# Ordering the start of an MLP's up projection by hand: features, operand sums and the first column pair of a Strassen-Winograd product

## The chip, the cores and the metric

One core of a Trainium2 chip runs the whole program. The metric is device microseconds of one execution. All matrix products are three matmuls each in a split format (see below), so that fp32 data keeps its precision.

## The reference, cut to what matters

A two-layer backbone over 1024 latent tokens and 256 context tokens, width 1024. Layer 0 mixes by differential attention, layer 1 by a bidirectional state-space layer with a gated linear unit (GLU). After every mixer stands a squared-ReLU MLP:

```python
x = x + g1 * rmsnorm(y_lat, norm_g[i, 1])
h = rmsnorm(x, norm_g[i, 2]) * (1.0 + s2) + sh2
x = x + g2 * rmsnorm(sqrelu_mlp(h, mlp_w1[i], mlp_w2[i]), norm_g[i, 3])

def sqrelu_mlp(h, w1, w2):
    return jnp.einsum('btf,fd->btd', jnp.square(jax.nn.relu(jnp.einsum('btd,df->btf', h, w1))), w2)
```

The change is in layer 1, where the context stream is no longer needed: the end of the GLU, the second norm, and the start of `h @ w1` (1024 tokens, 1024 to 4096).

## The kernel before, in words

**Formats.** `split` makes two fp32r halves of an fp32 tile: the high half on ScalarE (a copy, line 137), the low half as the difference on VectorE or GpSimd (line 138). `mm3` (lines 130 to 134) multiplies high by high, high by low and low by high.

**Tokens and columns.** Tokens come in two groups of 512 (g = 0, 1). The normalised activations are turned to features by rows: for each block k of 128 features, four TensorE transposes into one PSUM bank (line 315), a scaling with adaLN scale and shift on VectorE (320) or ScalarE (318), and a split (321, line 138 on GpSimd by default). The result is `hT[g]`, eight blocks each. The 4096 columns come in 32 columns f of 128. Columns 0 to 3 are computed directly (`conventional`: 8 blocks by 3 matmuls for each column and group). The other 28 go in 14 pairs p = 2 to 15 by a Strassen-Winograd scheme: 7 products of 4 blocks (12 matmuls) in place of 8. Its operands on the token side are sums of blocks of `hT`: T1 and T3, T2, and T4, which overwrites the first half of `hT[1]`. On the weight side they are four sums (S1 to S4).

**Order of a pair.** The products are A11·B11, S1·T1, S2·T2, S4·B22, S3·T3, A12·B21, A22·T4, in this order. A11·B11, S2·T2, S3·T3 and A22·T4 accumulate in one PSUM bank (P), S1·T1 and S4·B22 in another (R), A12·B21 in a third (Q). After A11·B11, S1·T1 and S2·T2 ScalarE copies the bank's state out (line 1428) before the next product is added to it. After the others VectorE adds the copy and squares (1432, 1433), or ScalarE takes ReLU and square (1397, 1398). The blocks of the result go to DRAM (Ad), and GpSimd forms four sums of them for the down projection (`sums`, lines 2086 to 2092).

**Scheduling.** Outside hand-ordered sections a scheduler decides at compile time the order of instructions on each engine, from the text's order as rank and a model of the times. Inside `with self.manual():` TensorE, VectorE, ScalarE and GpSimd each issue the section's instructions in the order of the text; where other instructions fall between them stays with the scheduler, and DMAs (all on SP's queue) are the scheduler's too. In before, this stage is all the scheduler's. `stages` and `advance` put the steps of the norm (`finish`, lines 2027 to 2045) between columns in the text.

**The stage.** `glu_done(1)` ends the GLU of the second group: norms, residual, norm, and the features. In before `second_group` (1334) emits for each i of 4 the features i and i + 4 and then the sums (1341 to 1350) that make T1, T3 and T2 of block i. `mlp1_up` (2063) does columns 0 to 3 for group 0, then loads and splits the same weights again for group 1 (2095 to 2103), then `last_sum` (1364) makes T4, four blocks of three VectorE sums and a split, then the pairs follow. `pair_weights` (1400) makes the weight sums and splits of a pair on VectorE and ScalarE; its scratch tile comes from a ring of two that `last_sum` uses too.

Of the kernel before, what the change touches and what calls it, by code (L numbers as in the profile page):

```python
# [70 lines left out]
class Prog:  # L71
# [236 lines left out]

    def to_feature(self, tiles, A, B, hi, lo, banks, tmps, k, eng=None, act=False):

        nc = self.nc
        b = banks.next()
        n = 128 * len(tiles)
        for i, t in enumerate(tiles):
            nc.tensor.transpose(b[:, 128 * i : 128 * i + 128], t[:, 128 * k : 128 * k + 128], self.ident)
        t = tmps.next()[:, 0:n]
        if act:
            nc.scalar.activation(t, b[:, 0:n], AF.Identity, scale=A[:, k : k + 1], bias=B[:, k : k + 1])
        else:
            nc.vector.tensor_scalar(t, b[:, 0:n], A[:, k : k + 1], B[:, k : k + 1], ALU.mult, ALU.add)  # L320
        self.split(hi[:, k, :], lo[:, k, :], t, eng or nc.gpsimd)
        return t
# [17 lines left out]
    def phase_v(self):  # L340
# [1039 lines left out]
    def halves(self, src, slot):  # L1380
        self.split(slot[:, 0], slot[:, 1], src)
        return slot
# [640 lines left out]
    def glu_done(self, g, y1, G, xs, tmps, tb):  # L2023
        nc = self.nc
        A, B = self.modc[:, 1, 4, 0], self.modc[:, 1, 3, 0]

        def finish(t, x):
            y, r = y1[t], [None, None]
            self.dma(x, self.xb[0].rearrange("(c t) d -> t c d", t=8)[t])

            def s0():
                r[0] = self.rms2(y, 4.0 * EPS)

            def s1():
                nc.vector.scalar_tensor_tensor(y, y, r[0], G, ALU.mult, ALU.mult)
                (nc.gpsimd if t % 2 else nc.vector).tensor_tensor(y, x, y, ALU.add)
                self.dma(self.xc[t], y)

            def s2():
                r[1] = self.rms2(y)  # L2040

            def s3():
                nc.scalar.activation(y, y, AF.Copy, scale=r[1])

            self.stages((s0, s1, s2, s3), 1)

        tiles = range(4 * g, 4 * g + 4)
        for t, x in zip(tiles, xs):
            finish(t, x)
        feature = lambda k, tmps: self.to_feature([y1[t] for t in tiles], A, B, *self.hT[g], tb, tmps, k, act=k % 2 == 1)  # L2050
        if g == 0:
            self.stages([lambda k=k: feature(k, tmps) for k in range(8)])
            return
        self.second_group(feature, Ring([self.fv(x, 512) for x in (40, 36, 38, 32, 34)]), 0)

# [7 lines left out]
    def mlp1_up(self):  # L2063
        nc = self.nc
        slots = [self.rv(x, 2, 512) for x in (56, 60, 64, 68, 72, 48, 52)] + [self.hv(64 + 4 * i, 2, 512) for i in range(4)]
        raw1 = Ring([self.wv(2 * i, 512) for i in range(4)])
        ring = Ring(slots[:8])
        banks = [0, 1, 2, 4, 5, 6, 7]
        mb = Ring([self.bank(i) for i in banks])
        ft, st = Ring([self.fv(2 * i, 512) for i in range(16)]), Ring([self.fv(32 + 2 * i, 512) for i in range(5)])  # L2070
        ss = Ring([self.fv(x, 512) for x in (42, 44)])
        put = lambda src: self.halves(src, ring.next())
        B = self.blocks()
        kept = {}

        def emit(p, j, g, t):
            kept[p, j, g] = t
            if (j, g) != (0, 1):
                self.dma(self.Ad[{(0, 0): 0, (1, 0): 5, (1, 1): 6}[j, g]][p], t)
            self.advance(2)  # L2080

        def sums(p, i):
            tt, a = nc.gpsimd.tensor_tensor, lambda j, g: kept[p, j, g]
            t = kept[p, i] = st.next()
            if i == 1:
                tt(t, a(0, 1), a(1, 1), ALU.add)
            elif i == 2:
                tt(t, kept[p, 1], a(0, 0), ALU.subtract)
            elif i == 3:
                tt(t, a(1, 0), kept[p, 2], ALU.subtract)  # L2090
            else:
                tt(t, a(0, 0), a(0, 1), ALU.subtract)
            self.dma(self.Ad[i][p], t)

        for g in range(2):
            if g:
                self.advance()
            for f in range(4):
                w = [put(r) for r in self.load1(1, f, raw1)]
                b, t = mb.next(), ft.next()  # L2100
                self.conventional(b, w, B, g)
                self.square(t, b)
                emit(f // 2, f % 2, g, t)
        self.last_sum(B, ss)
        ring = Ring(slots)
        for p in range(2, 16):
            if p == 15:
                ring = Ring(slots[3:7] + slots[:3])
            w = self.pair_weights([self.load1(1, 2 * p + j, raw1) for j in range(2)], put, ss.next(), False)
            if p == 15:  # L2110
                self.banks1 = [x for x in range(8) if x not in [banks[(mb.i + 1 + k) % 7] for k in range(3)]]
                self.mlp1_start()

            def out(j, g, t):
                emit(p, j, g, t)
                for i in {(0, 1): (), (1, 1): (1,), (0, 0): (2, 4), (1, 0): (3,)}[j, g]:
                    sums(p, i)

            self.pair_products(w, B, mb, [ft.next() for _ in range(4)], out)
            if p in (2, 3):  # L2120
                for i in (1, 2, 4, 3):
                    sums(p - 2, i)

    def mlp1_start(self):
# [235 lines left out]
```

## Time and profile before

| | |
|---|---|
| Time, three runs | 2892.81, 2894.29, 2899.42 us; median 2894.29 |
| The profiled execution's own time | 2899.15 us |
| Its span, first to last instruction | 2897.4 us |
| Mean granted TensorE clock | 0.982 |
| TensorE busy | 2747.0 us (95%), 15225 matmuls |
| VectorE busy | 2026.9 us (70%) |
| ScalarE busy | 1362.4 us (47%) |
| GpSimd busy | 1063.2 us (37%) |
| From 2263 to 2317 us: TensorE, VectorE, ScalarE, GpSimd busy | 42.32, 44.69, 30.31, 23.43 us of 54 |

The views of the profile used are the page's shares by engine, a table of busy time by stretch (us from the span's start, with the granted clock in a column), rows of single instructions in order of time, and the chain that ended last. A row of the timeline gives start, duration (both us), engine, line, operation, what is written from what, shape and count. In brackets stand the engine's idle time before it and what ended that idle time. DVE is VectorE, ACT ScalarE, POOL GpSimd, PE TensorE's matmuls; tiles are named by their pool (PS is PSUM, H, R, F and W are SBUF regions).

### The profile page before, as it was taken

The numbers are of one execution on the slowest core, as the hardware profiler recorded it, in microseconds if no ns is written. First come the engines' busy times: TensorE is split into PE (matmuls) and PEld (weight loads), VectorE is DVE, ScalarE is ACT, GpSimd is POOL, SyncE is SP. The second block draws the span as 40 slices with busy tenths as digits, with TensorE's granted clock in tenths as the row PEclk, the third lists the DMA queues.
The fourth block names the chain that finished last, engine by engine and source line by source line (L and its number), as shares of the span: only waits on it lengthen the run. The fifth ranks groups of instructions, "written<-read, shape, count | busy, mean of one in ns | idle before, by whom it ended". The sixth has DMA issues, their size and how long they took to land. (4 is left out here: it accounts for less than half of the span.)

```text
span 2897.4 us, 43677 instructions
## 1 busy us (share of the span) xinstructions
PE 2747.0 (95%) x15225; PEld 2296.1 (79%) x15225; DVE 2026.9 (70%) x2960; ACT 1362.4 (47%) x2555; POOL 1063.2 (37%) x923
## 2 busy tenths in 40 slices
PE   7999999999899999999999999789899899999999
PEld 4687888888787887878877778688788688878887
DVE  5456778878873667666788777899533787658466
ACT  3425555555654743333444435477344643344443
POOL 3314666666663600000110012699121543336324
PEclk9999999999999999999999999899999999999999
DMA  9955555555836468885899987579743254467544
GB/s 299 303 172 169 151 170 171 176 162 167 252 89 189 125 207 305 292 305 189 288 288 288 263 240 233 169 218 297 235 139 109 73 171 160 158 219 243 164 134 142
DMA packets 452010, 588.43 MB, mean 203 GB/s; under 512 B 60622, under 2 KB 297420, under 8 KB 448588
## 3 DMA queue, kind: packets, MB, share of 16 engines
q1 hardware_dynamic: 451788, 585.63, 64.1%
q8 instruction: 120, 1.97, 0.3%
q14 instruction: 102, 0.84, 0.1%
HBM read 398.47 MB, written 182.82 MB: 201 GB/s over the span
## 5 line engine op out<-in xcount | busy, mean ns | idle before, releaser
L132 PE MATMUL PS<-H 128*128 128x512 f32 x1048 | 413.8, 396 | 6.8 <-ACT H L137 3.9
L133 PE MATMUL PS<-H 128*128 128x512 f32 x1048 | 411.7, 393 | 0.0
L134 PE MATMUL PS<-H 128*128 128x512 f32 x1048 | 410.2, 392 | 0.0
L132 PE MATMUL PS<-H,R 128*128 128x512 f32 (+1 forms) x836 | 309.3, 375 | 0.7 <-ACT H L137 0.7
L133 PE MATMUL PS<-H,R 128*128 128x512 f32 (+1 forms) x836 | 304.9, 365 | 4.1 <-POOL H L138 4.1
L134 PE MATMUL PS<-H,R 128*128 128x512 f32 (+1 forms) x836 | 303.7, 364 | 0.0
L132 PEld LDWEIGHTS PS<-H 128*128 128x128 f32 x1048 | 198.4, 189 | 53.0 <-issue 4.9
L134 PEld LDWEIGHTS PS<-H 128*128 128x128 f32 x1048 | 198.3, 189 | 42.1 <-issue 0.4
L133 PEld LDWEIGHTS PS<-H 128*128 128x128 f32 x1048 | 198.7, 190 | 41.3 <-issue 1.0
L137 ACT ACTIVATE R<-W 128x512 fp32r<-128x512 f32 (+1 forms) x199 | 138.8, 705 | 181.7 <-PE PS L133 115.3
L546 ACT ACTIVATE F<-F,stat 128x1280 f32<-128x1280 f32 x128 | 174.3, 1362 | 100.6 <-DVE F L536 100.4
L132 PE MATMUL PS<-R,H 128*128 128x512 f32 x532 | 213.3, 403 | 1.6 <-ACT R L137 1.6
L133 PE MATMUL PS<-R,H 128*128 128x512 f32 x532 | 210.3, 395 | 0.0
L134 PE MATMUL PS<-R,H 128*128 128x512 f32 x532 | 208.5, 396 | 0.0
L137 ACT ACTIVATE H<-U 128x640 fp32r<-128x640 f32 x216 | 132.7, 676 | 148.4 <-PE PS L133 119.7
L138 DVE TENSOR_TENSOR H<-W,H 128x512 fp32r<-128x512 f32 (+1 forms) x137 | 126.9, 937 | 99.8 <-ACT H L137 99.8
L138 DVE TENSOR_TENSOR H<-U,H 128x640 fp32r<-128x640 f32 x216 | 166.4, 806 | 39.9 <-ACT H L137 38.9
L536 DVE TENSOR_SCALAR_CACHE_REDUCE F<-PS 128x1280 f32<-128x1280 f32 x128 | 185.2, 1483 | 8.1 <-PE PS L523 7.9
L138 DVE TENSOR_TENSOR R<-W,R 128x512 fp32r<-128x512 f32 (+1 forms) x164 | 146.7, 902 | 61.3 <-ACT R L137 54.1
L583 POOL TENSOR_SCALAR R<-F 128x256 fp32r<-128x256 f32 (+1 forms) x128 | 127.8, 999 | 148.8 <-ACT F L582 130.9
L133 PEld LDWEIGHTS PS<-H,R 128*128 128x128 f32 x836 | 161.0, 193 | 26.8 <-POOL H L138 5.9
L132 PEld LDWEIGHTS PS<-H,R 128*128 128x128 f32 x836 | 160.2, 192 | 26.5 <-issue 4.1
(501 smaller groups left out, 6843.4 us busy)
## 6 DMA issues: line engine op xcount, KB each, us to landing
W<-in_mlp_w SPq DMA_DIRECT2D x184, 256.0 KB, 3.2
U<-Aa SPq DMA_DIRECT2D x108, 320.0 KB, 4.2
Aa<-FU SPq DMA_DIRECT2D x91, 320.0 KB, 5.3
Ad<-F SPq DMA_DIRECT2D x112, 256.0 KB, 2.4
W<-Ad SPq DMA_DIRECT2D x112, 256.0 KB, 2.9
FU<-in_mlp_w SPq DMA_DIRECT2D x32, 512.0 KB, 5.9
Ta<-FU SPq DMA_DIRECT2D x16, 1024.0 KB, 4.3
recd<-U SPq DMA_DIRECT2D x64, 256.0 KB, 5.0
```

The source lines that it names most:

```text
L132: mm(out, ah, bh, start=first, stop=False, **kw)
L133: mm(out, ah, bl, start=False, stop=False, **kw)
L134: mm(out, al, bh, start=False, stop=last, **kw)
L137: self.nc.scalar.activation(hi, src, AF.Copy)
L138: (lo_eng or self.nc.vector).tensor_tensor(lo, src, hi.bitcast(F32), ALU.subtract)
L536: ts(p[c], self.PS[:, 1280 * c : 1280 * c + 1280], 1.0, None, ALU.mult, ALU.min, accum_out=sm[:, c : c + 1])
L546: nc.scalar.activation(p[c], p[c], AF.Exp, bias=sm[:, c : c + 1], scale=-1.0, accum_out=sn[:, 0:1] if c else s0[:, u + 1 : u + 2])
L583: nc.gpsimd.tensor_scalar(hi, t, 1.0, 0.0, ALU.mult, ALU.add)
```

## The change

Columns 0 to 3 of all tokens and pair 2 become one stretch of text, most of it ordered by hand.

- The weights of columns 0 to 3 are loaded and split once and kept in eight slots for both groups. Columns 0 to 2 of group 0 are multiplied ahead of the ordered section, column 3 inside it, between the first transposes of group 1.
- In the ordered section group 1's features come one after the other, 0 to 7. All are scaled on ScalarE, and their low halves are made on VectorE. Two features behind each, the products of block k for all four columns are issued, into four banks. From feature 4 on, T1 of block k − 4 and the fp32 sums for T2 and T3 are made; the splits of T2 come after the last feature.
- Then come pair 2's weights, ReLU and square of group 1's four columns, the splits of T3, `last_sum`, and pair 2's products with their evacuations; there the section ends.
- Rings of slots and tiles are reordered to fit. `second_group` stays for the first MLP only.

```diff
-        feature = lambda k, tmps: self.to_feature([y1[t] for t in tiles], A, B, *self.hT[g], tb, tmps, k, act=k % 2 == 1)
+        feature = lambda k, tmps: self.to_feature([y1[t] for t in tiles], A, B, *self.hT[g], tb, tmps, k,
+                                                  nc.vector if g else None, g == 1 or k % 2 == 1)
...
-        self.second_group(feature, Ring([self.fv(x, 512) for x in (40, 36, 38, 32, 34)]), 0)
+        self.feature1 = feature
...
-        for g in range(2):
-            if g:
-                self.advance()
-            for f in range(4):
-                w = [put(r) for r in self.load1(1, f, raw1)]
-                b, t = mb.next(), ft.next()
-                self.conventional(b, w, B, g)
-                self.square(t, b)
-                emit(f // 2, f % 2, g, t)
-        self.last_sum(B, ss)
-        ring = Ring(slots)
+        first = []
+        for f in range(4):
+            w, b = [put(r) for r in self.load1(1, f, raw1)], mb.next()
+            if f < 3:
+                self.conventional(b, w, B, 0)
+            first.append((w, b, ft.next()))
+            self.advance(2)
+        self.advance()
+        ring = Ring(slots[8:] + slots[0:8:2] + slots[1:8:2])
+        load = lambda p: [self.load1(1, 2 * p + j, raw1) for j in range(2)]
+        sched = self.manual()
+        sched.__enter__()
+        w = self.up_second(B, first, [mb.next() for _ in range(4)], [ft.next() for _ in range(4)], emit, ss,
+                           lambda: self.pair_weights(load(2), put, ss.next(), False))
         for p in range(2, 16):
...
+            if p > 2:
+                w = self.pair_weights(load(p), put, ss.next(), False)
...
             self.pair_products(w, B, mb, [ft.next() for _ in range(4)], out)
+            if p == 2:
+                sched.__exit__(None, None, None)
...
+    def up_second(self, B, first, banks, tiles, emit, ss, weights):
...
+        def t1(k):
+            t = more.next()
+            tt(t, raw[k], b11[k][0], ALU.subtract)
+            tt(t, t, b11[k][1], ALU.subtract)
+            self.split(T[1][0][:, k], T[1][1][:, k], t)
+            tt(raw[k], raw[k + 4], raw[k], ALU.subtract)
+            tt(raw[k + 4], raw[k + 4], t, ALU.subtract)
...
+        for k in range(8):
+            one(k)
+            for i in ((0, 1, 2), (3, 4, 5), (6, 7))[k] if k < 3 else ():
+                products(i, 0, [first[3][0:2]])
+            if k < 4:
+                relu(k)
+            if k > 3:
+                done(k - 4)
+            if k > 1:
+                products(k - 2)
+            if k > 3:
+                t1(k - 4)
+        halves(2, lambda k: raw[k + 4])
+        products(6)
+        products(7)
+        w = weights()
+        for f in range(4):
+            self.square(tiles[f], banks[f])
+            emit(f // 2, f % 2, 1, tiles[f])
+        halves(3, lambda k: raw[k])
+        self.last_sum(B, ss)
+        return w
```

`one(k)` makes feature k, `relu` and `done` are ReLU and square of group 0's columns, `products(k)` are 12 matmuls, and `halves(j, ...)` splits the four blocks of Tj.

More of the change, by code (lines that the diff above doesn't have):

```diff
@@ L2069, in mlp1_up @@
         mb = Ring([self.bank(i) for i in banks])
-        ft, st = Ring([self.fv(2 * i, 512) for i in range(16)]), Ring([self.fv(32 + 2 * i, 512) for i in range(5)])
+        ft, st = Ring([self.fv(2 * i, 512) for i in [0, 1, 2, 3, *range(8, 16), 4, 5, 6, 7]]), Ring([self.fv(32 + 2 * i, 512) for i in range(5)])
         ss = Ring([self.fv(x, 512) for x in (42, 44)])
         put = lambda src: self.halves(src, ring.next())
+        self.T = {j: (self.rv(16 * j - 16, 4, 512), self.rv(16 * j - 8, 4, 512)) for j in (1, 2, 3)}
         B = self.blocks()
@@ L2108, in mlp1_up @@
                 ring = Ring(slots[3:7] + slots[:3])
-            w = self.pair_weights([self.load1(1, 2 * p + j, raw1) for j in range(2)], put, ss.next(), False)
+            if p > 2:
+                w = self.pair_weights(load(p), put, ss.next(), False)
             if p == 15:
@@ L2122, in mlp1_up, with one, relu, done @@
                     sums(p - 2, i)
+    def up_second(self, B, first, banks, tiles, emit, ss, weights):
+        act, tt = self.nc.scalar, self.nc.vector.tensor_tensor
+        raw, free = {}, Ring([self.fv(x, 512) for x in (40, 36, 38, 32, 34, 8, 10, 12)])
+        more = Ring([self.fv(14, 512), self.fv(42, 512)])
+        b11 = [[t[:, k].bitcast(F32) for t in self.hT[0]] for k in range(4)]
+        T = self.T
+        def one(k):
+            raw[k] = self.feature1(k, free)
+        def relu(f):
+            act.activation(first[f][2], first[f][1], AF.Relu)
+        def done(f):
+            act.activation(first[f][2], first[f][2], AF.Square)
+            emit(f // 2, f % 2, 0, first[f][2])
+        def products(k, g=1, todo=[(f[0], b) for f, b in zip(first, banks)]):
+            x = B[f"B{k // 4 + 1}{g + 1}"]
+            for w, b in todo:
+                ah, al = (shaped(w[k // 4][:, j], (4, 128))[:, k % 4] for j in range(2))
+                self.mm3(b, ah, al, x[0][:, k % 4], x[1][:, k % 4], k == 0, k == 7)
+        def t1(k):
[5 more added lines that the diff above has]
+            tt(raw[k + 4], raw[k + 4], t, ALU.subtract)
+        def halves(j, src):
+            for k in range(4):
+                self.split(T[j][0][:, k], T[j][1][:, k], src(k))
+        for k in range(8):
[20 more added lines that the diff above has]
+        return w
     def mlp1_start(self):
```

## The prediction

> **What bounds the kernel.** I read the page first, then the busy time by stretch around the change, then the order of instructions there on TensorE, VectorE, ScalarE and GpSimd.
>
> ```profile
> span 2897.4 us, 43677 instructions
> ...
> PE 2747.0 (95%) x15225; PEld 2296.1 (79%) x15225; DVE 2026.9 (70%) x2960; ACT 1362.4 (47%) x2555; POOL 1063.2 (37%) x923
> ...
> core 0: us, PE busy (x) PEld busy (x) DVE busy (x) ACT busy (x) POOL busy (x), PEclk, DMA share, GB/s
> 2270.00:2285.00 15.00, 9.41 (x46) 6.80 (x47) 14.92 (x19) 10.65 (x20) 7.35 (x5) 1.00 0.57 175
> 2285.00:2300.00 15.00, 13.06 (x47) 9.88 (x46) 15.00 (x21) 7.40 (x13) 6.77 (x4) 0.77 0.00 1
> 2300.00:2315.00 15.00, 11.68 (x39) 9.05 (x38) 10.19 (x15) 7.43 (x14) 8.02 (x2) 0.77 0.10 33
> 2345.00:2375.00 30.00, 30.00 (x134) 24.86 (x133) 24.32 (x28) 11.19 (x20) 17.43 (x12) 1.00 0.57 199
> ```
>
> TensorE bounds the whole (95%). At 2345 it is full: 134 matmuls in 30 us. From 2270 to 2315 it issues 46, 47 and 39 in 15 us each, while VectorE is busy without a break until 2300, and the granted clock falls to 0.77. So in this stage VectorE is the bound, and the stage is the one that the change rewrites. TensorE's own rows:
>
> ```profile
> 2268.67 0.40 PE L134 MATMUL PS<-H 128*128 128x512 f32 x1
> ...
> 2283.91 0.66 PE L315 MATMUL PS<-ident,F 128*128 128x128 f32 x4 [3.36 <-DVE F L320]
> ...
> 2291.74 0.99 PE L315 MATMUL PS<-ident,F 128*128 128x128 f32 x4 [1.92 <-ACT F L318]
> ...
> 2306.47 0.80 PE L133 MATMUL PS<-H,R 128*128 128x512 f32 x1 [3.32 <-POOL H L138]
> ...
> 2307.49 0.63 PE L133 MATMUL PS<-H,R 128*128 128x512 f32 x1
> 2307.91 0.63 PE L134 MATMUL PS<-H,R 128*128 128x512 f32 x1
> ...
> 2312.18 0.50 PE L134 MATMUL PS<-H 128*128 128x512 f32 x1
> ...
> 2319.36 0.39 PE L132 MATMUL PS<-R 128*128 128x512 f32 x1
> ...
> 2322.08 0.39 PE L132 MATMUL PS<-R 128*128 128x512 f32 x1
> ```
>
> The first token half's four columns are done at 2268.9. At 2319.36 pair 2's second product (S1·T1, 12 matmuls) starts, at 2322.08 its third (S2·T2): 2.72/12 = 0.227 us each, so its first product began at 2316.64. Between 2268.9 and 2316.64 (47.7 us) TensorE has 96 matmuls (21.8 us) and eight sets of four transposes (0.44 us each by the chain's row below, 3.5 us) to do: 25.3 us. **22.4 us are lost here**: three long idles, shorter ones, and after each long one a stretch of matmuls 0.42 us apart (2307.49, 2307.91) instead of 0.227, after the last idle until 2312.18, 5.7 us that cost 2.7.
>
> **What the change removes.** The weights of the four columns are loaded and split once: 8 loads, 8 ScalarE and 8 VectorE instructions fall away. Eight low halves leave GpSimd for VectorE, four scalings leave VectorE for ScalarE. What GpSimd cost:
>
> ```profile
> 2263.36 1.29 POOL L138 TENSOR_TENSOR H<-F,H 128x512 fp32r<-128x512 f32 x1 [2.67 <-ACT H L137]
> ...
> 2284.59 1.60 POOL L138 TENSOR_TENSOR H<-F,H 128x512 fp32r<-128x512 f32 x1 [2.62 <-ACT H L137]
> 2284.97 1.77 DVE L1371 TENSOR_TENSOR F<-F,H 128x512 f32<-128x512 f32 x1
> ...
> 2297.51 8.91 POOL L138 TENSOR_TENSOR H<-F,H 128x512 fp32r<-128x512 f32 x1 [3.60 <-ACT H L137]
> ...
> 2299.20 0.68 DVE L1344 TENSOR_TENSOR F<-F,H 128x512 f32<-128x512 f32 x1
> 2299.80 0.68 DVE L138 TENSOR_TENSOR R<-F,R 128x512 fp32r<-128x512 f32 x1
> ```
>
> A VectorE sum beside a GpSimd one takes 1.77 instead of 0.68 us (1.1 lost), and one GpSimd subtraction took 8.91 us while VectorE ran sums every 0.60 us; TensorE's 3.32 us idle before 2306.47 waited for it. [...]
>
> **What it puts in.** Each engine now issues this stage, through pair 2, in the order of the text. That order is the point. I follow it with these durations:
>
> ```profile
> 2257.12 1.16 ACT L2043 ACTIVATE F<-F,stat 128x1024 f32<-128x1024 f32 x1 [0.36 <-POOL stat L144]
> ...
> 2259.07 0.44 PE PS L315 x4
> ...
> 2276.37 0.60 PE L315 MATMUL PS<-ident,F 128*128 128x128 f32 x4
> ...
> 2295.63 0.76 ACT L318 ACTIVATE F<-PS,modc 128x512 f32<-128x512 f32 x1
> 2296.29 0.62 ACT L137 ACTIVATE R<-W 128x512 fp32r<-128x512 f32 x1
> ...
> 2262.13 0.63 ACT L137 ACTIVATE R<-W 128x512 fp32r<-128x512 f32 x1 [1.63 <-DMA W<-in_mlp_w]
> ...
> 2262.79 0.69 DVE L138 TENSOR_TENSOR R<-W,R 128x512 fp32r<-128x512 f32 x1 [1.56 <-ACT R L137]
> ...
> 2270.00 0.64 ACT L1398 ACTIVATE F<-F 128x512 f32<-128x512 f32 x1
> 2270.52 0.60 ACT L1397 ACTIVATE F<-PS 128x512 f32<-128x512 f32 x1
> 2270.99 0.64 ACT L1398 ACTIVATE F<-F 128x512 f32<-128x512 f32 x1
> ...
> 2316.84 0.60 ACT L1428 ACTIVATE F<-PS 128x512 f32<-128x512 f32 x1 [0.58 <-PE PS L134]
> ```
>
> *Start.* The second group's last row is normalised at 2257.12 + 1.16 = 2258.3. TensorE is covered beyond that by columns 0 to 2: column 3 (24 matmuls, 5.4 us) now comes later, so the first transposes start at 2268.9 − 5.4 = 2263.5, 5.2 us after their input. Without that cover the wait would show.
>
> *Features.* Transposes 0 to 3 (1.8 us), column 3 (5.4) and the second half's products 0 and 1 (24 matmuls, 5.4) put transposes 4 at 2276.1. TensorE hardly waits up to here: one feature asks 0.66 + 0.52 + 0.48 us of ScalarE and 0.60 of VectorE, TensorE 2.5 or more. Feature 4's low half starts on VectorE after the transposes (0.60), scaling (0.76) and high half (0.62): 2278.1.
>
> *VectorE from there.* Up to the last sum for T4 it has four low halves, four times five instructions for T1 (k = 0 to 3; the sums for T2 and T3 are among them), four halves of T2, seven halves and four sums of pair 2's weights, four halves of T3, and 15 of last_sum: 58 × 0.60 = 34.8 us. Where a sum is split at once, VectorE waits for ScalarE's high half: 0.63 + 0.69 + two gaps of 0.03, less the 0.60 that is counted, 0.8 us. That is four times for T1, three for S1, S2 and S4, three for T4: 8.0 us. Before T3's halves ScalarE has the four squares of the second half: 8 instructions, 0.47 or 0.52 apart, 4.0 us. VectorE still has about 0.9 of low halves when they begin and needs a high half of 0.6 after them: 3.7 us idle. End: 2278.1 + 34.8 + 8.0 + 3.7 = 2324.6.
>
> *The new wait.* Pair 2's S2·T2 adds into the bank of A11·B11, so it waits for ScalarE's copy of that bank (L1428). In the text the copy stands behind last_sum. ScalarE must first do T4's fourth high half: 2324.6 + 0.1 + 0.5 = 2325.2, copy 0.6, S2·T2 at 2325.9. Queued behind it on TensorE are the other products of pair 2; behind the halves on VectorE the pair's evacuations. TensorE needs S2·T2 much earlier: the second half's products end near 2276.1 + 1.8 + 16.3 = 2294.2 (four more sets of transposes, 72 matmuls), A11's low half starts at 2278.1 + 28 × 0.60 + 4 × 0.8 = 2298.1, and A11·B11 and S1·T1 at first at the low clock end near 2305. About 20 us of TensorE are free there; those earlier stalls are hidden in it.
>
> [...]
>
> *What fills the wait.* Pair 3 stands outside the ordered section, and such work does get between ordered instructions: a copy of the next phase (L271) went ahead of the last instruction of the phase before, which is ordered by hand too (L1889).
>
> ```profile
> 2063.86 0.28 DVE L271 COPY adat<-PS 96x128 f32<-96x128 f32 x1
> 2064.05 0.68 DVE L1889 SCALAR_TENSOR_TENSOR H<-PS,H 128x512 fp32r<-128x512 f32 x1
> ...
> 2312.34 1.60 POOL L2086 TENSOR_TENSOR F<-F 128x512 f32<-128x512 f32 x1 [5.92 <-ACT F L1398]
> ...
> W<-in_mlp_w SPq DMA_DIRECT2D x184, 256.0 KB, 3.2
> ```
>
> Of pair 3 only A11·B11 and A12·B21 can run early: their weights need no sum, the raw buffers are free near 2303 and 2307 and filled 3.2 us later, and their halves fit the 0.8 us waits on VectorE. S1 can't: its scratch tile is last_sum's third. So 24 matmuls, 5.4 us, are brought forward. One sum for the Ad tiles (L2086) has both tiles and a free buffer by then and may run on GpSimd beside last_sum: 1.1 us on VectorE, so S2·T2 at 2327.0.
>
> *The low clock.* No row shows the clock after so long a wait with some work in it. Bounds: nothing, if the fill keeps the clock up, and 2.7 us, as after 2306.47. I take 2.4, near the upper end, as the granted clock is 0.77 in both stretches that hold the idles of 1.9 to 3.4 us. [...]
>
> **The sum.** S2·T2 later: 2327.0 − 2322.1 = +4.9. Low clock +2.4. Pair 3 brought forward −5.4. Net +1.9 us. TensorE is full behind this in before, and the rest isn't changed but for which slots and tiles are used. The profiled execution took 2899.15 us (span 2897.4), which is 4.9 above the median of 2894.29 of three runs (2892.81 to 2899.42); with +1.9 it would be 2901.1, and the median **2896**. So the stage gets rid of the GpSimd waits and pays them back in one long wait at pair 2. Under 0.2% (5.8 us) is about what a measurement here can't tell from no change.
>
> Bounds of this sum: transposes 0 could be placed before column 2 is done, at 2258.3, and everything would come 5.2 earlier (−3.3); pair 3 could bring nothing (+7.3). The GpSimd sums bunch behind pair 2: 15 by 1.6 us between its evacuations and pair 4's first copies; if VectorE or a buffer then waits, 0 to 3 us come on top.
>
> **Rivals.**
> *Faster: the copy isn't held.* If A11's copy gets out before T4's halves, S2·T2 follows S1·T1 near 2305 and only the last product, A22·T4, waits for T4's last low half, 2324.6 + 0.8 + 0.7 + 1.1 = 2327.2. In before it starts at 2316.64 + 72 × 0.227 = 2333.0. That is −5.8, with pair 3's two products −11.2, with the low clock −8.8: 2885.5. For it: a schedule is free to put other engines' work anywhere, and S2·T2 is wanted so early. Against it: the text orders ScalarE through pair 2.
>
> *Slower: nothing fills.* If pair 3's first halves are placed behind T4's, TensorE stands still for all 20 us: +7.3, 2901.6, with the bunched GpSimd sums up to 2905. It decides if A11's high half of pair 3 is on ScalarE after about 2324. For it: pair 3's loads queue on SP with the Ad stores, and these split halves are of lower rank than the ordered work. Against it: each of T4's halves comes 4 × 0.60 + 0.8 = 3.2 us after the one before and holds ScalarE for 0.52.
>
> *Not what it says:* GpSimd stays in the way, since the first group's halves still run there. The first of the rows above is the last one before the second group's; it ends at 2264.7, when VectorE has little to do: 1 us at most, inside the forecast.
>
> **Chances and range.** Forecast (−3.3 to +5) 0.50. Nothing fills, +5.8 to +11, 0.32: its cause needs only a different place for two splits. Copy not held 0.13, as the text speaks against it. A shorter chain or more filling than I see, past −5.8, 0.05. So faster 0.18, same 0.50, slower 0.32. The range from 2887 to 2905 leaves out most of the fast case and what lies beyond the bunched sums, 0.2 together.
>
> **What would show it.** In the trace after: transposes of the second group from about 2263; matmuls with few idles until about 2294; VectorE sums at 0.68 us with no GpSimd rows beside them; the first copy of pair 2 (the L1428 line's) on ScalarE directly behind the last half of T4; a TensorE idle of 5 us or more between pair 2's second and third products, with pair 3's first matmuls inside it; S2·T2 near 2327. If S2·T2 starts before 2315, the order is not what I read, and the forecast falls on the fast side. If VectorE has not the 58 instructions between feature 4 and T4's last sum, or they run at another pace than 0.60 us, the size is wrong by 1 us for each 0.017. If there is no pair 3 row in the wait, the slower case holds.

## The result, and the profile after

| | before | after |
|---|---|---|
| Time, median of 8 runs | 2893.55 us (2884.57 to 2899.42) | 2909.02 us (2901.12 to 2913.42) |
| Ratio | 1 | 1.0062, 95% interval 1.005 to 1.0075 |
| The profiled execution, span | 2899.15, 2897.4 us | 2905.57, 2903.6 us |

The change makes the kernel slower by 0.62%. The page of the kernel after:

```profile
span 2903.6 us, 43613 instructions
...
PE 2744.4 (95%) x15225; PEld 2292.5 (79%) x15225; DVE 2009.4 (69%) x2956; ACT 1363.5 (47%) x2551; POOL 1034.8 (36%) x915
```

Every engine but ScalarE (1363.5 us, 1362.4 before) is busy for less time than before, and the kernel takes longer, so this is a matter of waits. The two profiled spans differ by 6.2 us only, because the executions reach the stage at different times. The first transposes behind the GLU's last matmul start here, before and then after (TensorE's rows):

```profile
2241.41 1.03 PE L315 MATMUL PS<-ident,F 128*128 128x128 f32 x8
```

```profile
2235.14 1.03 PE L315 MATMUL PS<-ident,F 128*128 128x128 f32 x8
```

Over all profiled runs below this point lies between 2230.3 and 2246.6 us, for text ahead of it that the change doesn't touch. So I count from it, and write +80 for 80 us behind it. From it to the end are 656.0 us before and 668.5 us after: 12.5 us more. The stage after, busy time by stretch (us of the span; sums with instruction counts; the last three columns are granted clock, DMA share, GB/s):

```profile
core 0: us, PE busy (x) PEld busy (x) DVE busy (x) ACT busy (x) POOL busy (x), PEclk, DMA share, GB/s
2270.00:2285.00 15.00, 14.63 (x73) 11.76 (x72) 10.45 (x16) 7.75 (x13) 0.00 (x0) 1.00 0.21 71
2285.00:2300.00 15.00, 11.20 (x40) 8.17 (x39) 12.08 (x20) 7.06 (x12) 0.00 (x0) 0.89 0.10 35
2300.00:2315.00 15.00, 9.97 (x35) 7.03 (x33) 8.83 (x15) 10.15 (x19) 1.65 (x1) 0.89 0.38 123
2315.00:2330.00 15.00, 2.62 (x5) 1.66 (x6) 12.74 (x21) 5.15 (x9) 0.00 (x0) 0.54 0.05 17
2330.00:2345.00 15.00, 15.00 (x60) 12.21 (x59) 9.31 (x16) 5.87 (x11) 0.00 (x0) 0.89 0.30 87
2345.00:2375.00 30.00, 29.41 (x130) 24.02 (x128) 22.61 (x23) 9.09 (x16) 21.66 (x15) 1.00 0.60 210
2375.00:2400.00 25.00, 23.13 (x95) 18.95 (x96) 18.67 (x26) 8.76 (x15) 7.46 (x5) 0.93 0.45 150
```

The features are smooth now (73 matmuls in the first 15 us, 46 before). Then TensorE stands: 2.62 us busy from 2315 to 2330, at a clock of 0.54. Its rows around that hole, and a second, smaller one at pair 4:

```profile
2293.59 0.50 PE L132 MATMUL PS<-H 128*128 128x512 f32 x1 [2.44 <-ACT H L137]
...
2304.32 0.50 PE L132 MATMUL PS<-H,R 128*128 128x512 f32 x1 [2.02 <-ACT R L137]
...
2326.85 0.80 PE L132 MATMUL PS<-R 128*128 128x512 f32 x1 [14.87 <-ACT R L137]
...
2332.60 0.63 PE L134 MATMUL PS<-R 128*128 128x512 f32 x1
2333.03 0.57 PE L132 MATMUL PS<-R,H 128*128 128x512 f32 x1
...
2376.87 0.50 PE L132 MATMUL PS<-R 128*128 128x512 f32 x1 [2.46 <-ACT F L1428]
```

At 2293.59 pair 2's A11·B11 starts, at 2304.32 pair 3's A11·B11, and A12·B21 follows it. At 2326.85 pair 3's S1·T1 starts, after 14.87 us of idle time; it is 12 matmuls at the low clock (granted 0.50), 6.2 us for 2.7 of work, and only behind it, at 2333.03 (+97.9; before +80.7), comes pair 2's S2·T2. ScalarE shows why it was late:

```profile
2308.88 0.60 ACT L1428 ACTIVATE F<-PS 128x512 f32<-128x512 f32 x1 [0.93 <-PE PS L134]
...
2327.97 0.63 ACT L137 ACTIVATE H<-F 128x512 fp32r<-128x512 f32 x1
2328.51 1.07 ACT L1428 ACTIVATE F<-PS 128x512 f32<-128x512 f32 x2
...
2376.22 0.60 ACT L1428 ACTIVATE F<-PS 128x512 f32<-128x512 f32 x1 [6.81 <-POOL F L2094]
```

The copies of pair 2's A11 and S1 (the x2 row) stand directly behind the last high half of T4, at 2327.97, though A11·B11 had ended near 2299.6. This is the wait that the prediction described.

To compare kernels I use one measure throughout. **Lost time** is what each of TensorE's matmuls starts later than 0.227 us after the one before it (differences over 0.07 us), summed by stretch; the time of transposes is in it, mostly in the first stretch, and matters there only for differences.

| lost, us | +10 to +60 | +60 to +100 | +100 to +125 | +125 to +165 | +165 to +330 | +330 to +430 | sum | start of the stage to the end |
|---|---|---|---|---|---|---|---|---|
| before | 18.4 | 6.3 | 0.0 | 0.0 | 0.0 | 5.8 | 30.6 | 656.0 |
| after | 10.0 | 25.8 | 0.0 | 4.3 | 0.0 | 2.0 | 42.1 | 668.5 |
| e1_copies_first | 10.0 | 12.4 | 1.9 | 6.2 | 0.0 | 3.3 | 33.8 | 660.7 |
| e2_section_ends_early | 10.0 | 15.9 | 6.1 | 1.8 | 0.0 | 2.7 | 36.5 | 663.3 |
| e3_pair3_inside | 10.0 | 27.9 | 11.6 | 0.4 | 0.0 | 3.3 | 53.1 | 680.0 |
| e5_t3_ahead | 10.0 | 20.0 | 0.0 | 4.5 | 0.0 | 2.0 | 36.5 | 662.8 |
| e8_tiles_by_pair | 10.0 | 13.6 | 1.9 | 5.1 | 0.0 | 4.2 | 34.7 | 661.7 |
| e9_t3_too | 10.1 | 10.6 | 3.6 | 4.9 | 0.0 | 2.9 | 32.0 | 658.9 |
| e13_order_to_products | 8.1 | 12.0 | 2.5 | 1.7 | 0.0 | 3.6 | 27.9 | 654.7 |
| e12_no_hand_order | 5.0 | 14.4 | 5.2 | 0.4 | 0.0 | 4.1 | 29.1 | 655.5 |
| e6_weights_kept | 17.0 | 0.9 | 0.0 | 0.2 | 0.0 | 4.0 | 22.1 | 647.6 |
| e7_no_gpsimd | 16.1 | 0.0 | 0.0 | 0.0 | 0.0 | 6.1 | 22.2 | 647.4 |
| e11_both_parts | 12.2 | 0.0 | 0.1 | 0.0 | 0.0 | 5.9 | 18.3 | 643.7 |

The sums account for the last column's differences to before within 1.6 us. So of after's 12.5 us (11.6 by lost time): 8.4 gained in the features, 19.5 lost at pairs 2 and 3, 4.3 lost at pair 4, and 3.8 gained at a stop after +350, where TensorE waits for split halves on ScalarE.

### The profile page after: what moved, and what is told of

The parts are those of the page before. It is cut to its first block, busy times and chain, and to the rows that moved or that the text cites. A ratio compares the mean times of both kernels' runs of the same rounds, so it can differ in the third digit from the quotient of the medians.

```text
span 2903.6 us, 43613 instructions
## 1 busy us (share of the span) xinstructions
PE 2744.4 (95%) x15225; PEld 2292.5 (79%) x15225; DVE 2009.4 (69%) x2956; ACT 1363.5 (47%) x2551; POOL 1034.8 (36%) x915
## 5 line engine op out<-in xcount | busy, mean ns | idle before, releaser
L132 PE MATMUL PS<-H,R 128*128 128x512 f32 (+1 forms) x828 | 307.9, 374 | 2.7 <-ACT R L137 2.0
L133 PE MATMUL PS<-H,R 128*128 128x512 f32 (+1 forms) x828 | 299.6, 362 | 1.7 <-POOL H L138 1.4
L134 PE MATMUL PS<-H,R 128*128 128x512 f32 (+1 forms) x828 | 298.4, 362 | 0.0
L137 ACT ACTIVATE R<-W 128x512 fp32r<-128x512 f32 (+1 forms) x189 | 132.6, 710 | 178.1 <-PE PS L133 126.8
L137 ACT ACTIVATE H<-W 128x512 fp32r<-128x512 f32 (+2 forms) x160 | 97.2, 614 | 183.1 <-PE PS L133 129.4
```

Of the source, the lines that this page charges most:

```text
L132: mm(out, ah, bh, start=first, stop=False, **kw)
L133: mm(out, ah, bl, start=False, stop=False, **kw)
L134: mm(out, al, bh, start=False, stop=last, **kw)
L137: self.nc.scalar.activation(hi, src, AF.Copy)
```

## The experiments

The times below are ratios to the kernel before, each measured beside it on the same chip: a0 to e3 on one chip, e5 to e8 on a second, e11 to e13 on a third and e9 on a fourth. So between these groups the ratios are compared, not the times. Labels are those of the table.

**a0_after** is the kernel after once more, as the base of the next three.

> The changed kernel once more, to have its time beside the experiments on one chip. Both theories: 12 to 18 us above before. The profile of the change showed pair 2's S2·T2 97.9 us behind the last GLU matmul (80.7 in before); this should repeat within 1 us, while the time ahead of the GLU's end may differ by some us from run to run.

Measured: 1.0067 (1.0053 to 1.0081), 2908.17 us against 2889.88. The 15 us idle time and the stop at pair 4 are there again (25.5 and 4.4 us lost), and S2·T2 starts at +97.7.

**e1_copies_first** takes away the wait that the prediction named: the four blocks of `last_sum` are emitted behind the evacuations of pair 2's A11, S1, S2 and S4, in place of ahead of all.

```diff
-        self.last_sum(B, ss)
         return w
...
+            behind = {n: lambda k=k: self.last_sum(B, ss, (k,)) for k, n in enumerate(("A11", "S1", "S2", "S4"))} if p == 2 else {}
+            self.pair_products(w, B, mb, [ft.next() for _ in range(4)], out, behind)
```

> T4's four blocks are summed and split behind the evacuations of pair 2's A11·B11, S1·T1, S2·T2 and S4·B22 instead of ahead of all of them; nothing else is changed. Theory A (ScalarE's copies of pair 2 stand in line behind T4): S2·T2 starts about 67 us behind the last GLU matmul instead of 97.9, the 15 us idle goes, and only A22·T4 waits, to about 92; the kernel is 12 to 15 us faster than the changed one, so within 5 us of before. Rival B (VectorE has too much to do in the stage, whatever the order): the same instructions on VectorE, so no gain over the changed kernel, 12 to 18 us above before. Rival C (GpSimd's sums bunch at pair 4 and set the loss): 0 to 3 us better than the changed kernel.

Measured: 1.0054 (1.0036 to 1.0072). That is 3.8 us under a0 by the ratios, whose intervals overlap, 6.2 by the medians, and 7.8 under after by the last column of the table. TensorE's rows:

```profile
2313.48 0.50 PE L132 MATMUL PS<-R,H 128*128 128x512 f32 x1 [1.30 <-ACT F L1428]
...
2369.52 0.80 PE L132 MATMUL PS<-R 128*128 128x512 f32 x1 [4.04 <-ACT F L1428]
```

S2·T2 starts at 2313.48 (+76.4 from this run's 2237.10; +67 was expected), 21.5 us earlier than in after, and the 15 us idle time is gone: 13.4 us less are lost at +60 to +100 than in after. But some 5 us come back further on: the idle time at pair 4 is now 4.04 us, and VectorE has no room in the stretches ahead of it:

```profile
2327.10:2342.10 15.00, 13.40 (x58) 10.28 (x57) 15.00 (x23) 8.03 (x14) 2.82 (x2) 1.00 0.39 121
2342.10:2357.10 15.00, 13.35 (x59) 10.76 (x58) 14.97 (x13) 4.50 (x8) 12.44 (x9) 1.00 0.66 230
```

15.00 of 15 us, then 14.97 for only 13 instructions beside 12.44 us of GpSimd. So the wait was real, and taking it away is worth 4 to 8 us, a part of the loss; I had expected 12 to 15 by the theory that it is all of it. T4 itself is no earlier: its last high half comes at +94.8, in after at +92.8.

**e2_section_ends_early** ends the section in front of pair 2's products, so that their copies may be placed among T4's halves.

```diff
+            if p == 2:
+                sched.__exit__(None, None, None)
             self.pair_products(w, B, mb, [ft.next() for _ in range(4)], out)
-            if p == 2:
-                sched.__exit__(None, None, None)
```

> The ordered section ends ahead of pair 2's products instead of behind them, so the scheduler may put their copies between T4's halves. Theory A: S2·T2 starts near 67 us behind the last GLU matmul, T4 is ready at about 93, and the kernel is 10 to 13 us faster than the changed one. Rival B: no change from the changed kernel. Rival C: 0 to 3 us better.

Measured: 1.0056 (1.0038 to 1.0074). 9.6 us less are lost at +60 to +100 than in a0, and 6.1 appear behind; TensorE waits for VectorE and for ScalarE's halves at several places in place of one. ScalarE's rows, then one of TensorE:

```profile
2296.38 0.60 ACT L1428 ACTIVATE F<-PS 128x512 f32<-128x512 f32 x1
...
2333.61 0.63 ACT L137 ACTIVATE H<-F 128x512 fp32r<-128x512 f32 x1
```

```profile
2328.82 0.80 PE L132 MATMUL PS<-H,R 128*128 128x512 f32 x1 [4.49 <-ACT H L137]
```

The copy of A11 is out at once (2296.38, +64.3 from this run's 2232.03), and S2·T2 starts at +66.9, as expected. But T4's last high half, expected at +93, comes at 2333.61 (+101.6), 8.8 us later than in after, and now A22·T4 waits for T4. So with the copies free most of the loss by the ratio stays, and VectorE's chain up to T4 is what is late.

**e3_pair3_inside** moves pair 3 into the section, so that nothing of it can get between the ordered instructions.

```diff
-            if p == 2:
+            if p == 3:
                 sched.__exit__(None, None, None)
```

> The ordered section also takes in pair 3, so that no work of pair 3 can get between the instructions ahead of S2·T2. Theory D (pair 3's early work costs about what it brings, since its splits, sums and waiting copies stand in the ordered queues ahead of T4): T4's last high half comes about 6 us earlier, at 87 us behind the last GLU matmul instead of 92.8, no product of pair 3 runs in the wait, and the time is that of the changed kernel within 2 us. As predicted before the change was seen (the filling is free): T4 is not earlier, the three products are lost, and the kernel is 7 to 8 us slower than the changed one.

Measured: 1.0121 (1.0104 to 1.0139).

```profile
2335.57 0.80 PE L132 MATMUL PS<-R,H 128*128 128x512 f32 x1 [21.80 <-ACT F L1428]
```

ScalarE's last high half of T4:

```profile
2334.40 0.63 ACT L137 ACTIVATE H<-F 128x512 fp32r<-128x512 f32 x1 [2.81 <-DVE F L1372]
```

It comes at +87.8 (from 2246.63; +87 was expected, +92.8 in after), and S2·T2 at +88.9, against +97.9. So pair 3's instructions had held up S2·T2 by 9.0 us, 5.0 of them ahead of T4's last half. But TensorE idles 21.80 us with no filling, and then pair 3 waits for its own weights (11.6 us lost at +100 to +125). Both expected times missed (the same within 2 us, or 7 to 8 us more): the kernel is some 11 to 16 us slower than after. So the filling is worth more than its matmuls, since pair 3's halves and evacuations come late without it.

**e5_t3_ahead** puts T3's halves ahead of the squares.

```diff
+        halves(3, lambda k: raw[k])
         for f in range(4):
             self.square(tiles[f], banks[f])
             emit(f // 2, f % 2, 1, tiles[f])
-        halves(3, lambda k: raw[k])
```

> The changed kernel with the halves of T3 ahead of the four squares in the order by hand. VectorE idles 6.7 us in front of T3's low halves there, since ScalarE does eight instructions of the squares first (and three of pair 3 that got between). Theory A (the chain on VectorE up to T4 sets the wait of TensorE): T4's last high half and the first copy of pair 2 3 to 6 us earlier, TensorE's 15 us idle shorter by as much, total 3 to 6 us under the changed kernel. Theory B (pair 3's split halves and sums fill whatever gap opens, so that the chain stays as long): T4 within 1.5 us of where it was, total within 2.

Measured: 1.004 (1.0026 to 1.0055); 5.7 us less than after from the start of the stage to the end. T4's last high half comes at +87.9, 4.9 us earlier. TensorE's long idle time became 6.30 us, 5.8 us less are lost at +60 to +100. Theory A holds: as long as T4 stands ahead of the copies, VectorE's chain up to T4 sets TensorE's wait.

**e8_tiles_by_pair** is e1 with pair 4's tiles taken from those that the sums of pair 0 alone read, to price the stop at pair 4.

```diff
+        first, t8 = [], [ft.next() for _ in range(8)]
...
-            first.append((w, b, ft.next()))
+            first.append((w, b, t8[(0, 1, 4, 5)[f]]))
```

> As e1 (last_sum's blocks behind the evacuations of pair 2), and pair 4's product tiles are now those that the Ad sums of pair 0 alone read; in e1 and in the changed kernel two of them are also read by the sums of pair 1, which GpSimd does 10 to 20 us later. Theory A (the rest of the loss is the 4.0 us wait of pair 4's copy for GpSimd, and the low clock behind it): 4 to 6 us faster than e1, so 10 to 13 under the changed kernel and within 5 of the kernel before; no TensorE idle over 1 us around 132 us behind the GLU. Theory B (VectorE, busy 15.0 of 15 us in two stretches ahead of it, is what is late, and the wait only shows it): 0 to 1.5 us faster than e1, with a new wait for VectorE in the place of the old one.

Measured: 1.0029 (1.0018 to 1.004). The ratio is 0.25% better than e1's, but the intervals touch, and by its profile it loses 0.9 us more than e1 in all, with a stop of 3.21 us at pair 4 (4.04 in e1). ScalarE's rows, e1 first:

```profile
2364.05 0.63 ACT L137 ACTIVATE H<-F 128x512 fp32r<-128x512 f32 x1 [4.52 <-DVE F L1412]
...
2368.87 0.60 ACT L1428 ACTIVATE F<-PS 128x512 f32<-128x512 f32 x1 [2.52 <-POOL F L2096]
```

```profile
2362.78 0.63 ACT L137 ACTIVATE H<-F 128x512 fp32r<-128x512 f32 x1 [4.52 <-DVE F L1412]
...
2364.46 0.61 ACT L137 ACTIVATE R<-W 128x512 fp32r<-128x512 f32 x1
2364.98 0.57 ACT L1428 ACTIVATE F<-PS 128x512 f32<-128x512 f32 x1
```

The copy no longer waits 2.52 us for GpSimd, as meant. But in both the instructions ahead of it on ScalarE had waited 4.52 us for a weight sum (1412) on VectorE, and that wait stays. So by the trace theory B is nearer: behind the wait for GpSimd lies the late VectorE. By the ratios the gain is of theory A's size. What the tiles are worth by themselves is between 0 and some 7 us by the ratios, and isn't settled.

**e9_t3_too** adds T3's halves ahead of the squares to e8.

> e8 (last_sum's blocks behind pair 2's evacuations, pair 4's tiles by pair) with T3's halves ahead of the four squares as well, so all by hand still. Theory A (VectorE's chain still bounds the stage, so the 6.7 us that it waits in front of T3's halves still count): 3 to 5 us under e8, ratio to the kernel before about 1.0015, S1·T1's and S2·T2's waits of pair 2 unchanged or earlier, S3·T3 earlier. Theory B (with the copy no longer behind T4, GpSimd's sums of pairs 0 to 3 and pair 4's copy set the end, and these start when pair 2's evacuations are done): within 1.5 us of e8.

Measured: 1.0027 (1.0015 to 1.0039), the same as e8 within what can be told, as theory B has it; the profiled run is 2.8 us under e8's from the start of the stage to the end, nearly theory A's 3, so the two aren't told apart. No version ordered by hand to the end of pair 2 is better, and it is slower than before.

**e13_order_to_products** keeps the section around the features and the columns' products only, and **e12_no_hand_order** has no section at all; the text is that of after in both. e13 opens the section at the loop over the features in `up_second` and closes it behind `products(7)`; what both take away is:

```diff
-        sched = self.manual()
-        sched.__enter__()
...
-            if p == 2:
-                sched.__exit__(None, None, None)
```

> The changed kernel with the section by hand only around the eight features and the second half's products: pair 2's weights, the squares, T3, last_sum and pair 2's products are placed freely. Theory A (the loss is made behind the products, by the order of weights, squares, T3 and T4): as the version with no hand order, 12 to 25 us under the changed kernel. Theory B (it is made in the features, where T1's sums and the transposes alternate by the text): 4 to 8 us under the changed kernel, as where the section ended just ahead of pair 2's products (2.8 us under it).

> The changed kernel, its text and its order of the sums by operand unchanged, with the section ordered by hand taken away: the instructions are placed as everywhere else in the phase. Theory A (the order by hand makes the loss): 15 to 28 us under the changed kernel, ratio to the kernel before 0.994 to 1.001; no TensorE idle of over 5 us at pair 2 or pair 3. Theory B (the sums by operand make it: T1, then T2, weights, T3 put T3 and T4 late whoever orders them): within 6 us of the changed kernel, TensorE idle before pair 2's second or third product.

Measured: e13 1.0014 (1.0005 to 1.0024), e12 1.001 (0.9996 to 1.0023). So with the section gone the kernel is as fast as before within what can be told, some 13 to 16 us under after, and nearly all of that comes back if the section ends behind the columns' products. The order by hand costs its price behind the features; around them it costs nothing that shows in the whole. As e2, whose section ends in front of pair 2's products, is still at 1.0056, most of the price lies in weights, squares, T3 and T4. In e12 a wait of 6.25 us at pair 2 stays (ahead of +64.8), where theory A had none over 5, so not all of the loss in the stage is the order by hand.

**e6_weights_kept** and **e7_no_gpsimd** are the kernel before with one part of the change each: the split weights kept, and the second group scaled on ScalarE with low halves on VectorE. **e11_both_parts** has the two.

```diff
-                w = [put(r) for r in self.load1(1, f, raw1)]
+                if g == 0:
+                    first[f] = [put(r) for r in self.load1(1, f, raw1)]
+                w = first[f]
```

```diff
-tb, tmps, k, act=k % 2 == 1)
+tb, tmps, k, nc.vector if g else None, g == 1 or k % 2 == 1)
```

> The kernel before with the first columns' split weights kept for both token halves, and nothing else of the change: eight loads, eight high halves on ScalarE and eight low halves on VectorE fewer. Theory A (VectorE bounds the stage there, so its eight instructions of 0.60 us count): 2 to 5 us under the kernel before. Theory B (these halves lie in gaps that exist anyway, as VectorE idles 4.8 us of 15 from 2300 to 2315): within 1.5 us of it.

> The kernel before with the second token half scaled on ScalarE and its low halves on VectorE, and nothing else of the change: no GpSimd subtraction in the stage. Theory A (the 3.3 us TensorE wait for the 8.9 us GpSimd subtraction and the 1.1 us that each GpSimd sum costs a VectorE sum go): 3 to 7 us under the kernel before. Theory B (VectorE, which bounds the stage, gets eight low halves for four scalings, +2.4 us): 1 to 4 us over it.

> The kernel before with both parts that were faster alone: the split weights kept (e6, ratio 0.9981) and the second token half scaled on ScalarE with its low halves on VectorE (e7, 0.9969); no order by hand, T1 to T3 column by column as before. Theory A (the two take away different waits): ratio to the kernel before about 0.995, 12 to 16 us less. Theory B (both remove the same waits, TensorE's idles at features): about 0.997, no better than e7 alone. The kernel after minus this one is the price of the rest of the change, the order by hand and the sums by operand: 24 to 32 us under theory A.

Measured: e6 0.9981 (0.9969 to 0.9993), e7 0.9969 (0.9955 to 0.9983), e11 0.9978 (0.9965 to 0.999). Each part makes the kernel faster, e7 by 9.6 us (2880.02 against 2889.59). By the table the two add up partly (sum of lost time 22.1, 22.2 and 18.3), by the ratios e11 isn't better than e7; which of the two is the best kernel is open. All three beat before and after.

e11 and e12 make the same sums and splits; e12's text has them by operand, and the columns' products by block k in place of column by column, with the banks and the rings of slots and tiles to go with it. By the ratios that text costs 0.3% (1.001 against 0.9978), some 9 us, and 11.8 us by the last column of the table. VectorE's counts suggest where it goes. The first 45 and the next 47 us of the stage, in after, e12 and e11:

```profile
2235.14:2280.14 45.00, 42.48 (x213) 34.36 (x212) 15.45 (x20) 26.15 (x45) 16.83 (x16) 1.00 0.12 42
2280.14:2327.14 47.00, 25.95 (x95) 18.91 (x94) 34.87 (x55) 22.18 (x39) 1.65 (x1) 0.81 0.18 62
```

```profile
2230.30:2275.30 45.00, 43.80 (x219) 35.97 (x218) 16.64 (x23) 29.78 (x52) 16.94 (x16) 1.00 0.16 59
2275.30:2322.30 47.00, 37.28 (x149) 29.22 (x148) 41.63 (x67) 24.66 (x44) 12.86 (x3) 0.89 0.23 75
```

```profile
2241.80:2286.80 45.00, 39.28 (x198) 31.16 (x197) 21.54 (x32) 31.54 (x55) 16.87 (x16) 1.00 0.16 59
2286.80:2333.80 47.00, 45.97 (x202) 37.65 (x203) 45.03 (x68) 27.62 (x48) 9.11 (x6) 1.00 0.32 103
```

By +92 VectorE has issued 100 instructions in e11, 90 in e12 and 75 in after, and TensorE 400, 368 and 308. In the first 45 us after gives TensorE more work than e11 does (213 against 198), and VectorE 20 instructions against 32: the sums by operand begin only with feature 4, those by column follow each pair of features i and i + 4. VectorE is the bound of what follows, and after leaves it idle for 29.6 of these 45 us. T4's last sum starts at +68.5 in e11, +77.8 in before, +86.6 in e12 and +92.1 in after. By 2291.15 (2293.59 less 2.44; +56) TensorE has used up the columns' products there, and all that follows needs VectorE's sums; e11, with its columns still to do, has 0.0 us lost at +60 to +100. That the rest of the text makes the difference is shown by e11 and e12, but not which part of it: the order of the sums, that of the products, the banks and the rings were not tried one by one. That the early idle time of VectorE is how it does so is read from these rows, and no run tested it alone.

## Why the prediction was wrong, step by step

The kind of wait was right, and its place: features with few stops, the ScalarE copy behind T4, the wait of S2·T2, pair 3 inside it, GpSimd's sums bunched at pair 4. A loss was forecast too, but one of 1.9 us, and the medians differ by 15.5; the sizes are what failed. **The step that failed is the time of T4 and of S2·T2 behind it, with pair 3's filling counted as gain only**: S2·T2 was forecast at 2327.0, which is +85.6 in the count from the stage's start, and measured at +97.9. Of the 12.3 us, T4's last high half has 9.5 (forecast +83.3, measured +92.8), and the rest lies behind it. VectorE's rows in after:

```profile
2273.67 0.69 DVE L138 TENSOR_TENSOR H<-F,H 128x512 fp32r<-128x512 f32 x1 [2.52 <-ACT H L137]
2274.28 0.69 DVE L2158 TENSOR_TENSOR F<-F,H 128x512 f32<-128x512 f32 x1
2275.00 0.69 DVE L2159 TENSOR_TENSOR F<-F,H 128x512 f32<-128x512 f32 x1
...
2278.32 0.69 DVE L138 TENSOR_TENSOR H<-F,H 128x512 fp32r<-128x512 f32 x1
...
2301.98 1.89 DVE L138 TENSOR_TENSOR R<-W,R 128x512 fp32r<-128x512 f32 x3
...
2310.55 1.29 DVE L138 TENSOR_TENSOR R<-F,R 128x512 fp32r<-128x512 f32 x2 [2.87 <-ACT R L137]
2312.02 0.69 DVE L1432 TENSOR_TENSOR F<-PS,F 128x512 f32<-128x512 f32 x1 [0.17 <-PE PS L134]
...
2314.66 0.68 DVE L1433 SCALAR_TENSOR_TENSOR F<-F 128x512 f32<-128x512 f32 x1
...
2325.45 0.69 DVE L1407 TENSOR_TENSOR F<-W 128x512 f32<-128x512 f32 x1
```

- *Start:* feature 4's low half at +38.5 (2273.67), forecast +36.7: 1.8 late. Most of it lies ahead of the ordered section: at +13.4 TensorE idled 1.40 us for a GpSimd low half of the first group (row below), where before has no such stop. The first transposes came at +17.4, near the early bound of the prediction, but what follows came no earlier for it.
- *Pace:* a T1 block takes 4.65 us (2273.67 to 2278.32), not 4.4. A sum that reads what the sum just ahead of it wrote started 0.72 us behind it here (2274.28, 2275.00), not 0.60. Four blocks: 1.0 late. The 58 instructions were counted right.
- *T3's wait:* 6.7 us from the end of pair 2's last low half (2303.87) to 2310.55, forecast 3.7. Two splits of pair 3 and its copy at 2308.88 stand among the squares on ScalarE: 3.0 late. In e3, without them, the wait is 4.2. e5 showed that this wait counts.
- *last_sum:* 17.4 us from 2310.55 to T4's last high half, forecast 13.9: 3.5 late. Pair 3's sums and weight sums (1432, 1433, 1407, 1409) stand between its instructions, and its own sums wait for one another. In e3 it takes 14.9.
- *Behind T4:* the copy ends at 2329.1, and S2·T2 starts 3.9 us later, as pair 3's S1·T1 at the low clock was put ahead of it. 1.1 was forecast for a GpSimd sum beside last_sum; that sum ran at 2311.32, and two low halves on VectorE beside it took 1.50 us in place of 1.29. So 2.8 late in all.

```profile
2248.55 0.50 PE L133 MATMUL PS<-H,R 128*128 128x512 f32 x1 [1.40 <-POOL H L138]
```

The difference to e3 prices pair 3: 2.5 us in T3's wait, 2.5 in last_sum and about 4 behind T4, which makes the 9.0. The rest is the chain's own: 1.8 at the start, 1.0 in T1, 0.5 in front of T3's halves and 1.0 in last_sum, less the 1.1 that didn't come, makes 3.2. The prediction counted the filling as gain only; its instructions on the ordered engines also delayed the ordered chain, by these 9.0 us.

- *Pair 3 brought forward:* forecast two products, 5.4 us; there were three, 8.2, with S1·T1 too. S1's scratch tile is last_sum's third, as predicted, but that block was done at 2324.93, and S1's sum went in at 2325.45, among the fourth's instructions. I also read before wrongly. Its rows, TensorE and then VectorE:

```profile
2313.91 0.39 PE L132 MATMUL PS<-H,R 128*128 128x512 f32 x1
...
2316.64 0.39 PE L132 MATMUL PS<-H,R 128*128 128x512 f32 x1
```

```profile
2319.84 0.68 DVE L1432 TENSOR_TENSOR F<-PS,F 128x512 f32<-128x512 f32 x1
```

ScalarE's copy at 2316.84 takes what ended there, so A11·B11 began at 2313.91. What began at 2316.64 is A12·B21, whose add (1432) follows at 2319.84. So 12 more matmuls are ahead of S2·T2 in before than I counted, its 22.4 us of lost time are 19.7, and as the text puts A12·B21 behind S2·T2, the net of what was brought forward is 5.4 again.

- *Low clock:* forecast 2.4 behind S2·T2; it was 3.5 (one short wait included), ahead of it, in pair 3's S1·T1.
- *Sum for the stage:* forecast +1.9. Measured: S2·T2 17.2 later than in before, less 5.4, is +11.8; by the lost time +11.1.
- *Pair 4:* 0 to 3 forecast on top, as a bound; 4.3 measured, 2.46 of them idle time and the rest low clock behind (granted 0.53 from 2377.67 to 2381.32). ScalarE's copy at 2376.22 waited 6.81 us for GpSimd's sum, and GpSimd itself had waited 3.17 us for the store of an earlier sum.
- *The gain of the parts:* in the features 8.4 us are gained, as forecast in kind. e6 and e7 show that the parts bring 0.2 to 0.3% with the text of before; in e12, with the new text, nothing of that is left.
- *Rivals:* the fast one fell with the rows of ScalarE. The slow one gave 2901.6 to 2905 and named the wrong mechanism: the wait was filled. Its price was too low as well: in e3, where nothing fills, 24.0 us more than in before pass from the start of the stage to the end, against its 7.3.

What stays open: the medians differ by 15.5 us, the two profiled runs by 12.5 from the stage's start to the end. 3 us are within what the time ahead of the stage varies from run to run. Which part of the new text makes VectorE late isn't settled either.

## What to carry to other kernels

When a stage is bound by one engine, ask first when that engine's chain starts, and how much of the other engine's work is left to cover it. Here TensorE gained 8.4 us early and lost 19.5 later, behind a VectorE that was idle for 29.6 of the first 45 us. The order by hand held pair 2's copies on ScalarE behind T4 until 2328.51, though A11·B11 had ended near 2299.6, while pair 3's work from outside still slipped in between. So count for each filling instruction what it delays as well as what it brings, and see whether copies that free a bank stand behind a long chain; moving them alone gave 4 to 8 us, while the chain stayed as late. Try the parts of a change alone: two of this one's were 0.2 to 0.3% faster under the scheduler's own order.

## What the runs showed of the hardware that I had not expected

**The low clock came late behind a stop of 2.02 us, and not at all behind one of 2.24.** In after, TensorE idled 2.02 us ahead of 2304.32. Its first six matmuls behind that started within 1.8 us, 0.23 to 0.39 apart, at a granted clock of 1.00, before 3.4 us of them were 0.42 us apart (2306.10 to 2309.50, granted clock 0.50). The idle time had begun 2.9 us behind another slow stretch (2296.08 to 2299.40, granted clock 0.52). The length of the idle time alone doesn't settle it. The same product of pair 2 waited as long in e1 and in e8, first and second row:

```profile
2318.74 0.50 PE L132 MATMUL PS<-H,R 128*128 128x512 f32 x1 [2.24 <-ACT F L1428]
```

```profile
2317.47 0.50 PE L132 MATMUL PS<-H,R 128*128 128x512 f32 x1 [2.23 <-ACT F L1428]
```

In e1 the matmuls behind it started 0.22 to 0.24 us apart from 2319.07 to 2321.38, as in after at a granted clock of 1.00 (2299.40 to 2302.30). In e8 they started 0.42 to 0.43 us apart from 2318.56 to 2321.55, as in after at 0.50. What decides between the two is open.

**One GpSimd sum took 10.13 us beside a VectorE that hardly paused.** In e12, one GpSimd sum, of a kind that takes 1.26 to 1.75 us in after (2311 to 2376), took 10.13 us, and VectorE then waited for a weight load behind it (GpSimd's row, then VectorE's):

```profile
2290.17 10.13 POOL L2088 TENSOR_TENSOR F<-F 128x512 f32<-128x512 f32 x1 [38.84 <-DVE F L2157]
```

```profile
2305.35 0.69 DVE L1407 TENSOR_TENSOR F<-W 128x512 f32<-128x512 f32 x1 [4.50 <-DMA W<-in_mlp_w]
```

The sum ended at 2300.3; VectorE had run some 40 instructions 0.60 us apart on average from 2275.3 to 2299.26, and one beside its end took 1.59 us; that the load waited for this sum was not tried.
